# An attention-and-SwiGLU encoder layer on one core: adaLN partly on TensorE in the first wave, looser places for projection tiles, the last chunk's o tiles at other addresses

## The chip, the core and the metric

The kernel runs on one core of a Trainium2 chip. The core has five engines that run at the same time: TensorE (PE, matrix products; its weight loads are listed apart as PEld), VectorE (DVE), ScalarE (ACT), GpSimd (POOL) and SyncE (SP, which here only issues DMAs). They work on SBUF (128 partitions) and on PSUM, which has eight banks of 128 x 512 float32; PE writes PSUM. The metric is the device time of one execution in microseconds, the median of several runs.

## The reference, cut to what matters

One encoder layer: 2048 tokens of 1024 features, float32. A vector c is turned into six shift, scale and gate vectors; windowed attention and a SwiGLU FFN follow, each between two RMS norms.

```python
c_act = silu(c)
sh1, sc1, g1, sh2, sc2, g2 = split(c_act @ ada_w + ada_b, 6)
h = rmsnorm(x, mix_norm_pre) * (1 + sc1) + sh1
y = windowed_gqa_sink(h, w_qkv, w_o, sink, rel_bias)   # 16 heads, 4 kv heads, window 128
x = x + g1 * rmsnorm(y, mix_norm_post)
h = rmsnorm(x, ffn_norm_pre) * (1 + sc2) + sh2
a, b = split(h @ ffn_w_in, 2)                          # 2816 hidden
x = x + g2 * rmsnorm((silu(a) * b) @ ffn_w_out, ffn_norm_post)
```

## The kernel before, in words

The tokens lie along the free dimension in four chunks of 512; the 1024 features are eight tiles of 128 partitions (index k). Each float32 operand of a large product is split into a high part (a cast to a shorter float format, `hi`) and a rest (`lo`), and one product becomes three: hi·hi, hi·lo, lo·hi (`three`).

The order of stages is: a **first wave** for chunk 0, in which seven of the twelve 128-column groups of q, k and v are accumulated at once in seven PSUM banks over k; the other groups, chunk 1; then 64 attention units (4 chunks, 4 kv heads, 4 blocks of 128 queries), between which products of the q, k, v projection (first 32 units) and of the output projection for chunks 0 to 2 (last 32 units) are spread as filler; the output projection of the last chunk; then the FFN, by a Strassen-like scheme with seven products for two by two blocks. In the profile `k,q` are score products, `ident,pr` transposes of the probabilities, `phi,v` and `plo,v` value products, `ol,wo` output projection, `hb,w..`/`ht,w..` FFN.

For the first wave, each k needs a shift and a scale column (`mod`). Each column is one DVE reduction over a 128 x 1024 tile of ada_w against silu(c) broadcast to all partitions (`cb`); then x is multiplied by the norm factor r (`nr`), scaled and shifted on ACT, cast to `hi` on ACT, and `lo` is the difference on DVE. The weights come in raw tiles from a pool of five (`raws`), which the ada_w tiles share.

The program is not issued as written. A recorder (`Recorder`) takes all operations; a list scheduler (`forward`, `backward`, several rounds) orders them on each engine by its own estimates and gives each tile a place, and `emit` issues that order, so that all operations carry the line of `emit`. Tiles of one pool and tag share a number of places. `slot_of` gives a place only to the tile whose turn it is in the order in which the program first used the tag's tiles:

```python
t = b.tag
if t.order[t.next] is not b:
    return None
```

So with two places for (`psF`, `mm`), which hold output projections (`py`) and norm sums (`nst`) alike, a norm sum that is not ready holds up all projections behind it. After attention, SBUF that its pools had is given to the last chunk's output projection (`lasto`), from the top of the right side down in the order in which the pools are opened; attention's own pools began there with the bias tables, then q, k, v. A tile waits for the last reader of whatever lay at its address.

## Time and profile before

| | us |
|---|---|
| median of 3 runs | 2035.23 (2032.91 to 2036.42) |
| the profiled execution | 2033.44 |
| its span, first to last instruction | 2031.6 |
| PE busy | 1995.9 (98%) |
| DVE busy | 1689.8 (83%) |
| ACT busy | 1072.0 (53%) |
| POOL busy | 571.7 (28%) |

The chain that ended last is 65% PE. A group's or row's busy time counts overlapping matmuls once; a single matmul row is longer than the distance between two starts, because each drains while the next one runs. Rows of the timeline give start, length, engine, line, operation, tiles and shapes, and in brackets the idle time before it with what ended it.

### The profile page before, as it was taken

The page shows a single profiled execution, that of the slowest core. Times are in us where ns is not written, and L with a number is a line of the kernel's source. Part 1 is how long each engine was busy: PE and PEld are TensorE (multiplying, and loading weights), DVE is VectorE, ACT ScalarE, POOL GpSimd, SP SyncE. Part 2 cuts the span into 40 slices and gives each one's busy share as a digit, 9 for nine tenths or more (in the row PEclk, how much of TensorE's full clock was granted, in tenths as well). Part 3 has the DMA queues.
Part 4 walks back from the last instruction along what each step waited for, and adds up shares of the span by engine and source line. Part 5 has one row for each costly group of instructions (what it writes and reads, how often), then busy time and mean ns, then how long its engine had stood idle before and what let it go on. Part 6 is the DMA issues. An engine that isn't in the chain of part 4 may idle for free.

```text
span 2031.6 us, 29024 instructions
## 1 busy us (share of the span) xinstructions
PE 1995.9 (98%) x9392; PEld 1663.1 (82%) x9392; DVE 1689.8 (83%) x3051; ACT 1072.0 (53%) x2099; POOL 571.7 (28%) x520
## 2 busy tenths in 40 slices
PE   6999999999999999999999999999999999999999
PEld 4888888888787878788888888888888888888888
DVE  7868888877989888988887998776776789989997
ACT  5557766777778864344343533333333744455433
POOL 1302442344657513432333231111111000120034
PEclk9999999999999999999999999999999999999999
DMA  9895765576777694444446743333233794398543
GB/s 312 307 331 198 241 210 173 195 279 227 254 272 257 225 363 152 160 161 165 166 158 244 272 151 134 117 137 106 83 124 101 236 335 152 108 331 300 174 156 110
DMA packets 208581, 415.23 MB, mean 204 GB/s; under 512 B 19964, under 2 KB 61997, under 8 KB 205357
## 3 DMA queue, kind: packets, MB, share of 16 engines
q1 hardware_dynamic: 207852, 412.84, 59.1%
q8 instruction: 75, 1.23, 0.2%
q14 instruction: 78, 0.63, 0.1%
q10 hardware_dynamic: 576, 0.52, 0.1%
HBM read 278.52 MB, written 134.77 MB: 203 GB/s over the span
## 4 chain that ended last, share of the span: by engine, by line
PE 65%; DVE 2%; DMA 1%; issue 1%; ACT 0%; POOL 0%; SPq 0%; ACTq 0%; DVEq 0%; POOLq 0%
PE bank L748 65%; DMA hb<-h_d 0%; DVE pr L748 0%; DMA wor<-w_o 0%; DVE u_i L748 0%; DVE y L748 0%; DVE plo L748 0%; DMA ly<-y_d 0%; DMA lx<-xT 0%; DVE ly L748 0%; POOL ly L748 0%; DVE ws_i L748 0%; DVE wa_i L748 0%; SPq L748 0%; DVE of L748 0%
## 5 line engine op out<-in xcount | busy, mean ns | idle before, releaser
L748 PE MATMUL bank<-ht,ws_i 128*128 128x512 f32 x1584 | 374.0, 389 | 0.0
L748 PEld LDWEIGHTS bank<-ht,ws_i 128*128 128x128 f32 x1584 | 297.3, 188 | 61.7
L748 PE MATMUL bank<-hb,wa_i 128*128 128x512 f32 x1056 | 254.1, 389 | 0.5 <-DVE hb L748 0.5
L748 PEld LDWEIGHTS bank<-hb,wa_i 128*128 128x128 f32 x1056 | 198.1, 188 | 42.0 <-DVE hb L748 0.9
L748 PE MATMUL bank<-ol,wo 128*128 128x512 f32 x768 | 206.1, 396 | 2.1 <-ACT yacc L748 1.1
L748 DVE TENSOR_TENSOR u_i<-bank,u_i 128x512 f32<-128x512 f32 x176 | 120.9, 688 | 80.3 <-PE bank L748 77.7
L748 ACT CAST ws_i<-s_i 128x512 fp32r<-128x512 f32 x132 | 81.9, 621 | 192.9 <-DVE s_i L748 96.8
L748 ACT ACTIVATE pr<-pr,nm 128x385 f32<-128x385 f32 (+1 forms) x256 | 154.8, 606 | 53.2 <-DVE nm L748 48.0
L748 DVE CUSTOM_DVE_ANT_0 pr<-bank,bias,nsink 128x384 f32<-128x384 f32 (+1 forms) x256 | 149.8, 594 | 25.3 <-PE bank L748 21.7
L748 POOL TENSOR_SCALAR pr<-pr,rs 128x384 f32<-128x384 f32 (+1 forms) x177 | 114.6, 660 | 179.7 <-DVE rs L748 167.9
L748 PEld LDWEIGHTS bank<-ol,wo 128*128 128x128 f32 x768 | 141.2, 188 | 28.5 <-ACT yacc L748 1.5
L748 POOL TENSOR_TENSOR p_i<-p_i,u_i 128x512 f32<-128x512 f32 x41 | 66.9, 1633 | 346.3 <-DVE u_i L748 176.0
L748 POOL TENSOR_TENSOR z<-z,z 128x512 f32<-128x512 f32 x28 | 43.8, 1572 | 337.4 <-ACT ws_o L748 263.2
L748 PE MATMUL bank<-k,q 128*128 128x384 f32 (+1 forms) x512 | 135.4, 344 | 1.5 <-DVE nm L748 1.4
L748 PE MATMUL bank<-hi,ws 128*128 128x512 f32 x384 | 134.3, 400 | 0.0
L748 DVE TENSOR_TENSOR plo<-bank,phi 128x512 fp32r<-128x512 f32 x184 | 120.7, 684 | 11.2 <-ACT phi L748 10.1
L748 ACT CAST wa_i<-wiri 128x512 fp32r<-128x512 f32 x132 | 81.3, 620 | 90.8 <-PE bank L748 77.6
L748 PE MATMUL bank<-hb,ws_i 128*128 128x512 f32 x528 | 126.9, 389 | 1.6 <-ACT p_i L748 1.6
L748 PE MATMUL bank<-ht,wa_i 128*128 128x512 f32 x528 | 126.8, 389 | 0.0
L748 DVE TENSOR_TENSOR z<-bank,z 128x512 f32<-128x512 f32 (+1 forms) x164 | 107.7, 659 | 17.9 <-PE bank L748 16.5
L748 DVE TENSOR_TENSOR wa_i<-wiri,wa_i 128x512 fp32r<-128x512 f32 x132 | 103.8, 788 | 19.1 <-ACT wa_i L748 19.1
L748 PEld LDWEIGHTS bank<-hb,ws_i 128*128 128x128 f32 x528 | 99.0, 188 | 22.5 <-ACT p_i L748 2.0
(275 smaller groups left out, 4434.5 us busy)
## 6 DMA issues: line engine op xcount, KB each, us to landing
wiri<-w_in SPq DMA_DIRECT2D x88, 512.0 KB, 4.6
ada<-ada_w SPq DMA_DIRECT2D x40, 512.0 KB, 5.3
q_d<-e SPq DMA_DIRECT2D x32, 512.0 KB, 4.6
q<-q_d SPq DMA_DIRECT2D x16, 1024.0 KB, 7.0
wo<-wo_d SPq DMA_DIRECT2D x16, 1024.0 KB, 6.0
wiro<-w_out SPq DMA_DIRECT2D x40, 384.0 KB, 4.4
g_d_b<-p_i SPq DMA_DIRECT2D x44, 256.0 KB, 3.4
g_d_t<-p_i SPq DMA_DIRECT2D x40, 256.0 KB, 2.0
```

The costliest lines, as they stand in the source:

```text
L748: o.ins = getattr(engs[o.eng], o.fn)(*args, **kw)
```

## The change

- **First wave.** c also comes as eight columns (`ct`). For k = 0 the shift and the scale column are made by PE, eight products of one column each (`ada_products`, from a transposed copy of that part of ada_w), into a PSUM tile, and DVE adds the bias. The other k keep the DVE reduction. The ada_w tiles of the wave get a pool of their own with ten places (`raws0`), at the address of the second half of the weights, which opens after the wave. The split of the first half of the weights goes to DVE in the program instead of POOL. For chunk 0, `hi` is written by the scaling activation itself, the norm sum takes four partial sums instead of three, and its refinement is the short form (three DVE operations).
- **Warm products.** `busy` puts 14 products of 128 columns on `ones` at the start of PE's queue, six after the first partial sum, five on `t` and eight on `r` of the norm; nothing reads their result.
- **Loose places.** A tile may take a place ahead of up to four others of another name family (the leading letters of its name) for (`psF`, `mm`) and (`yp`, `nsq`). The y tiles of chunks 0 to 2 have 16 places instead of 12.
- **Last chunk.** The three pools of `lasto` are opened in another order: the o tiles first, so that they lie where the bias tables and the first q tiles lay, then weights, then y.

```diff
+ADA_PE = 1
+WARM = {"ones": 14, 0: 6, "t": 5, "r": 8}
+LOOSE = {("psF", "mm"): 4, ("yp", "nsq"): 4}
...
+            t.left = list(t.order)
+            skip = LOOSE.get((t.pool.name, t.name), 0)
+            t.reach = skip + 1
...
-            if t.order[t.next] is not b:
+            for x in t.left[:t.reach]:
+                if x is b:
+                    break
+                if x.family == b.family:
+                    return None
+            else:
                 return None
...
             for i, sq in enumerate(sums):
                 pe.matmul(ps, f(ones), sq, start=i == 0, stop=i == len(sums) - 1)
+                if fill is not None:
+                    fill(i, sq)
...
-            dve.tensor_tensor(sq[6], sq[4], sq[6], ALU.add)
-            self.acc = [sq[0], sq[2], sq[6]]
+            self.acc = sq[::2]
...
+            if c == 0:
+                act.activation(hi, xt, AF.Identity, bias=mod[:, k:k + 1], scale=coef[:, 0, k:k + 1])
+            act.activation(xt, xt, AF.Identity, bias=mod[:, k:k + 1], scale=coef[:, 0, k:k + 1])
+            if c == 0:
+                return scaled, dve.tensor_tensor(lo, xt, f(hi), ALU.subtract)
...
+        def ada_products(k):
+            for e, t in enumerate((8 + k, k)):
+                w = raws0.tile([P, D], F32, tag="raw", name=f"adat{t}")
+                sp.dma_start(w, a["ada_t"][t])
+                j = 2 * k + e
+                for i in range(KT):
+                    pe.matmul(ada_ps[:, j:j + 1], w[:, i * P:(i + 1) * P], ct[:, i:i + 1],
+                              start=i == 0, stop=i == KT - 1)
+                dve.tensor_tensor(mod[:, t:t + 1], ada_ps[:, j:j + 1], adab[:, t:t + 1], ALU.add)
...
-            split(t[:, 0], t[:, 1], w[:, :n], pool)
+            split(t[:, 0], t[:, 1], w[:, :n], pool if i else dve)
...
+        def busy(what, src):
+            for _ in range(WARM.get(what, 0)):
+                pe.matmul(warm[:, :P], f(ones), src[:, :P], start=True, stop=True)
...
-                y = yp.tile([P, CH], F32, tag="y", name=f"y{c}_{n}", bufs=4 if c == NCH - 1 else 12)
+                y = yp.tile([P, CH], F32, tag="y", name=f"y{c}_{n}", bufs=4 if c == NCH - 1 else 16)
...
+    op = open_pool(lasto, "op3", 4, side="right")
+    wop = open_pool(lasto, "wop3", 2, side="right")
     yp = open_pool(lasto, "yp3", side="right")
-    wop = open_pool(lasto, "wop3", 2, side="right")
-    op = open_pool(lasto, "op3", 4, side="right")
```

Since the scheduler orders everything anew, the change moves instructions on every engine. Three places follow.

PE at the very start, before (`nsq` are partial sums of squares, `hi` and `w` the operands of the first wave):

```order
L748 MATMUL bank0<-nsq0_0_86,ones_57 128x512
L748 MATMUL bank0<-nsq0_2_95,ones_57 128x512
L748 MATMUL bank0<-nsq0_6_115,ones_57 128x512
L748 MATMUL bank1<-hi0_0_164,w0_0_137 128x512
L748 MATMUL bank2<-hi0_0_164,w0_0_137 128x512
```

and now:

```order
L767 MATMUL bank0<-ones_57 128x128 x14
L767 MATMUL bank1<-nsq0_0_103,ones_57 128x512
L767 MATMUL bank0<-nsq0_0_103,ones_57 128x128 x6
L767 MATMUL bank1<-nsq0_2_114,ones_57 128x512
L767 MATMUL bank1<-nsq0_4_128,ones_57 128x512
L767 MATMUL bank1<-nsq0_6_138,ones_57 128x512
L767 MATMUL bank2<-mod_64,adat8_105 128x1 x8
L767 MATMUL bank2<-mod_64,adat0_112 128x1 x8
L767 MATMUL bank0<-nta0_175,ones_57 128x128 x5
L767 MATMUL bank0<-nr0_154,ones_57 128x128 x8
L767 MATMUL bank3<-hi0_0_206,w0_0_173 128x512
```

Sixteen one-column products and 13 warm ones now stand between the norm sum and the first product of the wave.

DVE in the same place, before, from the last sum of squares to the first `x` times r (`nr`; ISA rows on ada tiles are the reductions):

```order
L748 TENSOR_TENSOR nsq0_6_115<-nsq0_4_105,nsq0_6_115 128x512
L748 ISA ada8_93,mod_132<-ada8_93,cb_84,adab_88 128x1024
L748 ISA mod_132 128x1
L748 ISA ada0_98,mod_132<-ada0_98,cb_84,adab_88 128x1024
L748 ISA mod_132 128x1
L748 TENSOR_TENSOR w0_0_137<-wqkv0_0_103,w0_0_137 128x896
L748 SCALAR_TENSOR_TENSOR nta0_143<-bank0,nta0_143 128x512
L748 ISA ada1_113,mod_132<-ada1_113,cb_84,adab_88 128x1024
L748 ISA mod_132 128x1
L748 TENSOR_SCALAR nta0_143<-nta0_143 128x512
```

and now:

```order
L767 TENSOR_TENSOR mod_64<-bank2,adab_101 128x1
L767 SCALAR_TENSOR_TENSOR nta0_175<-bank1,nr0_154 128x512
L767 SCALAR_TENSOR_TENSOR nta0_175<-nta0_175,nr0_154 128x512
L767 SCALAR_TENSOR_TENSOR coef_186<-mod_64,gains_131 128x1
L767 SCALAR_TENSOR_TENSOR nr0_154<-nta0_175,nr0_154 128x512
L767 TENSOR_TENSOR w0_0_173<-wqkv0_0_119,w0_0_173 128x896
L767 TENSOR_TENSOR x0_0_71<-x0_0_71,nr0_154 128x512
L767 TENSOR_TENSOR mod_64<-bank2,adab_101 128x1
L767 ISA ada9_136,mod_64<-ada9_136,cb_126,adab_101 128x1024
L767 ISA mod_64 128x1
L767 ISA ada1_141,mod_64<-ada1_141,cb_126,adab_101 128x1024
L767 ISA mod_64 128x1
```

Three reductions no longer stand among the norm's steps; an add that reads PE's modulation bank stands ahead of them, and two reductions follow `x` times r.

PE in the second half of attention, around the norm of chunk 0's new x (`nhix0`; `wo1_n` are projection tiles of chunk 1), before:

```order
L748 MATMUL bank7<-plo9_3_2_5721,v2_3_5120 128x512
L748 MATMUL bank4<-ident_59,pr10_3_5513 128x128
L748 MATMUL bank5<-ident_59,pr10_3_5513 128x128
L748 MATMUL bank6<-ident_59,pr10_3_5513 128x128
L748 MATMUL bank3<-k3_0_5308,q3_0_5301 128x384 x2
L748 MATMUL bank2<-k3_0_5308,q3_0_5301 128x384 x2
L748 MATMUL bank1<-nhix0_5747,ones_57 128x512
L748 MATMUL bank0<-ol1_0_4217,wo1_4_5528 128x512 x4
```

and now:

```order
L767 MATMUL bank0<-ol1_3_5126,wo1_4_5548 128x512 x3
L767 MATMUL bank1<-ol1_0_4261,wo1_5_5671 128x512 x6
L767 MATMUL bank1<-ol1_1_4281,wo1_5_5671 128x512 x3
L767 MATMUL bank3<-k3_0_5363,q3_0_5353 128x384 x2
L767 MATMUL bank1<-ol1_1_4281,wo1_5_5671 128x512 x3
L767 MATMUL bank5<-ident_59,pr10_3_5574 128x128 x2
L767 MATMUL bank6<-ident_59,pr10_3_5574 128x128 x2
L767 MATMUL bank4<-ident_59,pr10_3_5574 128x128
L767 MATMUL bank1<-ol1_2_5097,wo1_5_5671 128x512
L767 MATMUL bank2<-k3_0_5363,q3_0_5353 128x384 x2
L767 MATMUL bank1<-ol1_2_5097,wo1_5_5671 128x512 x2
L767 MATMUL bank0<-nhix0_5837,ones_57 128x512
```

Projection tile 4 and most of tile 5 have moved ahead of the norm sum.

PE after attention's last value product (`plo15_3_1`; `ol3_n` are the last chunk's o tiles, `hb` the FFN's), before:

```order
L748 MATMUL bank7<-plo15_3_1_7249,v3_3_6684 128x512
L748 MATMUL bank0<-ol2_2_6043,wo2_6_7032 128x512
L748 MATMUL bank0<-ol2_3_6068,wo2_6_7032 128x512 x6
L748 MATMUL bank1<-ol2_0_5132,wo2_7_7174 128x512 x6
L748 MATMUL bank1<-ol2_1_5218,wo2_7_7174 128x512 x6
L748 MATMUL bank1<-ol2_2_6043,wo2_7_7174 128x512 x6
L748 MATMUL bank1<-ol2_3_6068,wo2_7_7174 128x512 x6
L748 MATMUL bank0<-ol3_0_7136,wo3_0_6868 128x512 x6
```

and now:

```order
L767 MATMUL bank7<-plo15_3_1_7328,v3_3_6769 128x512
L767 MATMUL bank1<-ol2_1_5271,wo2_7_7050 128x512 x3
L767 MATMUL bank1<-ol2_2_6070,wo2_7_7050 128x512 x6
L767 MATMUL bank1<-ol2_3_6101,wo2_7_7050 128x512 x6
L767 MATMUL bank0<-ol3_0_6628,wo3_0_7268 128x512 x6
```

Fewer products of chunk 2 are left for after attention. From the last row shown to the first product on `ol3_3` there are 36 more products before and 31 now: 73 and 52 in all.

More of the change, by code (lines that the diff above doesn't have):

```diff
@@ L2 @@
 import random
+import re
 from contextlib import ExitStack
@@ L92, in __init__ @@
         self.log, self.ops, self.slot, self.real = [], set(), None, None
+        self.group, self.family = None, re.match("[a-z]*", name).group()
 class Tag:
@@ L193, in record @@
             op.reads.append(op.writes[0])
-        elif fn == "matmul":
+        elif fn == "matmul" and op.writes[0][0].group is None:
             op.writes = [(op.writes[0][0], (3, (1 << P) - 1))]
@@ L218, in record @@
                     op.tiles.append(b)
+        if eng == "pe" and op.writes[0][0].group is not None:
+            for q in op.writes[0][0].group:
+                op.pred.setdefault(q, 0)
+            op.writes[0][0].group = [op]
         op.succ = []
@@ L262, in cost @@
             elif outs[0].dtype == F32 and ins[0].dtype == F32:
-                op.occ, op.lat = 860 * n // CH, 1060 * n // CH
+                op.occ, op.lat = max(860 * n // CH, 230), max(1060 * n // CH, 400)
             else:
@@ L545, in forward @@
                     t.next += 1
+                    t.left.remove(b)
                     wake(t)
@@ L754, in f, with columns @@
     return ap.bitcast(F32)
+def columns(nc, ap):
+    b = nc.bufs[ap.tensor.name]
+    b.unit, b.group = 1, []
 def row(ap, n):
@@ L800, in encoder_layer @@
     gains = constr.tile([P, 4, KT], F32, name="gains")
+    ct = mod[:, 6 * KT:7 * KT]
     nsink = const.tile([P, HEADS], F32, name="nsink")
@@ L808, in encoder_layer, with rstd_of @@
     pool.custom(lambda nc, t: make_identity(nc, t), ident)
-    def rstd_of(alloc, psp, ptag, acc, tag, r=None, direct=False, short=False, keep=False):
+    def rstd_of(alloc, psp, ptag, acc, tag, r=None, direct=False, short=False, keep=False, fill=None):
         sums = acc if isinstance(acc, list) else [acc]
@@ L834, in rstd_of @@
             dve.scalar_tensor_tensor(out, t, 1.5, r, ALU.add, ALU.mult)
+            if fill is not None:
+                fill("t", t)
+                fill("r", r)
             return out
@@ L889, in squares0, with norm @@
                     dve.tensor_tensor(sq[k - 1], sq[k - 1], sq[k], ALU.add)
-            dve.tensor_tensor(sq[6], sq[4], sq[6], ALU.add)
-            self.acc = [sq[0], sq[2], sq[6]]
-        def norm(self, psp, ptag):
+            self.acc = sq[::2]
+        def norm(self, psp, ptag, fill=None):
             r = nrm.tile([P, CH], F32, tag="nr", name=f"nr{self.c}")
-            self.r = rstd_of(rot(nrm, "nsq", 2), psp, ptag, self.acc, f"a{self.c}", r)
+            self.r = rstd_of(rot(nrm, "nsq", 2), psp, ptag, self.acc, f"a{self.c}", r,
+                             short=self.c == 0, fill=fill)
         def h(self, k):
@@ L899, in h @@
             scaled = dve.tensor_tensor(xt, xt, self.r, ALU.mult)
-            act.activation(xt, xt, AF.Identity, bias=mod[:, k:k + 1], scale=coef[:, 0, k:k + 1])
             hi = hs.tile([P, CH], F32R, tag="hi", name=f"hi{c}_{k}")
@@ L937, in encoder_layer @@
     with ExitStack() as pa:
-        w2 = open_pool(pa, "w2", side="right")
         raws = open_pool(pa, "raws", 5, side="right")
         w1 = open_pool(pa, "w1", side="right")
+        first = ExitStack()
+        raws0 = open_pool(first, "raws0", KT * C2 * 2 // D, side="right")
         psA = open_pool(pa, "psA", 8, space=PSUM)
         cb = nrm.tile([P, D], F32, name="cb")
+        sp.dma_start(ct, a["ct"])
         sp.dma_start(cb, row(a["c"], D))
@@ L947, in encoder_layer @@
         sp.dma_start(gains, a["gains"])
+        act.activation(ct, ct, AF.Silu)
         act.activation(cb, cb, AF.Silu)
@@ L957, in ada_reduce @@
             dve.tensor_tensor_reduce(w, w, cb, 1.0, adab[:, t:t + 1], ALU.mult, ALU.add, mod[:, t:t + 1])
+        ada_ps = psA.tile([P, CH], F32, tag="mm", name="ada_ps")
+        columns(nc, ada_ps)
+        def ada_products(k):
[7 more added lines that the diff above has]
+                dve.tensor_tensor(mod[:, t:t + 1], ada_ps[:, j:j + 1], adab[:, t:t + 1], ALU.add)
         wres = {}
         def w_piece(k, i):
-            pl, lo_c, n = ((w1, 0, C1), (w2, C1, C2))[i]
+            pl, lo_c, n = (w2, C1, C2) if i else (w1, 0, C1)
             w = raws.tile([P, D], F32, tag="raw", name=f"wqkv{k}_{i}")
@@ L970, in w_piece @@
                 wres[k, "v"] = (t[:, 0, :2 * P], t[:, 1, :2 * P])
+        warm = psA.tile([P, CH], F32, tag="mm", name="warm")
+        def busy(what, src):
+            for _ in range(WARM.get(what, 0)):
+                pe.matmul(warm[:, :P], f(ones), src[:, :P], start=True, stop=True)
+        busy("ones", f(ones))
         ch0.squares0()
-        ch0.norm(psA, "mm")
+        ch0.norm(psA, "mm", busy)
         steps = []
@@ L976, in encoder_layer @@
         for k in range(KT):
-            ada_reduce(*ada_load(8 + k, raws))
-            ada_reduce(*ada_load(k, raws))
+            if k < ADA_PE:
+                ada_products(k)
+            else:
+                ada_reduce(*ada_load(8 + k, raws0))
+                ada_reduce(*ada_load(k, raws0))
             dve.scalar_tensor_tensor(coef[:, 0, k:k + 1], mod[:, 8 + k:9 + k], 1.0, gains[:, 0, k:k + 1],
@@ L984, in encoder_layer @@
                 three(pss[n], wres[k, n], ch0.hh[k], k == 0, k == KT - 1)
+        first.close()
+        w2 = open_pool(pa, "w2", side="right")
         for n in NORD[:WAVE]:
@@ L1833 @@
         "ada_w": np.asarray(ada_w)[0].T.reshape(6 * KT, P, D),
+        "ada_t": np.asarray(ada_w)[0].reshape(KT, P, 6 * KT, P)[:, :, :KT + ADA_PE].transpose(2, 1, 0, 3)
+        .reshape(KT + ADA_PE, P, D),
+        "ct": np.asarray(c).reshape(KT, P).T,
         "ada_b": cols(ada_b[0]),
```

## The prediction

> **What bounds the kernel now.** I read the page's first part, then what PE waited for, then engine times by stretches cut at those waits, then the timeline at each.

> ```profile
> span 2031.6 us, 29024 instructions
> PE 1995.9 (98%) x9392; PEld 1663.1 (82%) x9392; DVE 1689.8 (83%) x3051; ACT 1072.0 (53%) x2099; POOL 571.7 (28%) x520
> ...
> PE bank L748 <- DVE nsq L748: 9.1, 3, 5.8
> PE bank L748 <- ACT hi L748: 8.1, 1, 8.1
> PE bank L748 <- DVE lo L748: 3.1, 2, 2.4
> ...
> 0.00:23.40 23.40, 6.19 (x7) 1.51 (x7) 12.45 (x24) 14.91 (x19) 2.04 (x7) 1.00 0.92 329
> 23.40:26.40 3.00, 3.00 (x7) 2.29 (x8) 3.00 (x4) 1.69 (x2) 1.59 (x1) 1.00 0.70 194
> 26.40:66.00 39.60, 36.35 (x152) 28.89 (x152) 35.52 (x49) 20.75 (x30) 14.95 (x8) 0.96 0.88 287
> 66.00:540.00 474.00, 472.68 (x2514) 405.79 (x2513) 384.68 (x902) 332.67 (x740) 162.51 (x199) 1.00 0.71 241
> 540.00:565.00 25.00, 21.98 (x100) 16.99 (x99) 21.46 (x51) 16.09 (x38) 18.38 (x16) 0.86 0.87 288
> 565.00:630.00 65.00, 65.00 (x349) 55.93 (x348) 55.98 (x140) 53.99 (x122) 34.38 (x43) 1.00 0.72 238
> 630.00:660.00 30.00, 28.03 (x149) 22.35 (x148) 29.65 (x73) 24.88 (x63) 24.89 (x28) 1.00 0.90 299
> 705.00:717.00 12.00, 9.47 (x38) 6.61 (x37) 10.17 (x15) 7.78 (x13) 0.59 (x1) 1.00 1.05 405
> 717.00:1990.00 1273.00, 1271.44 (x5604) 1051.53 (x5604) 1069.94 (x1659) 546.02 (x965) 269.59 (x176) 1.00 0.52 181
> ```

> In the stretches the columns are length, busy time of PE, PEld, DVE, ACT and POOL, PE's granted clock, DMA share and GB/s. From 66 us on TensorE is the bound, so time is to be had only where it idles or runs slowly. It idles 1.3 us in 66 to 540, 3.0 in 540 to 565, nothing to 630, 2.0 to 660, 2.5 in 705 to 717, and 1.6 in the 1273 us after. The start is the large piece:

> ```profile
> 8.47 3.21 ACT L748 ACTIVATE nsq<-x 128x512 f32<-128x512 f32 x5 [2.35 <-DMA x<-xT]
> 13.29 2.04 PE L748 MATMUL bank<-nsq,ones 128*128 128x512 f32 x2 [1.33 <-DVE nsq L748]
> 14.09 1.28 DVE L748 CUSTOM_DVE_ANT_0 ada<-ada,cb,adab 128x1024 f32<-128x1024 f32 x1 [0.95 <-ACT cb L748]
> 15.30 0.08 DVE L748 DVE_READ_ACCUMULATOR2_ANT mod<- 128x1 f32 x1
> 15.37 0.69 ACT L748 ACTIVATE nr<-bank,epsc 128x512 f32<-128x512 f32 x1
> 16.84 0.63 ACT L748 ACTIVATE nr<-nr 128x512 f32<-128x512 f32 x1
> 16.96 1.09 DVE L748 TENSOR_TENSOR w<-wqkv,w 128x896 fp32r<-128x896 f32 x1 [0.37 <-ACT w L748]
> 18.16 0.69 DVE L748 SCALAR_TENSOR_TENSOR nta<-bank,nta 128x512 f32<-128x512 f32 x1
> 21.89 0.81 ACT L748 ACTIVATE x<-x,mod,coef 128x512 f32<-128x512 f32 x1
> 23.40 3.25 PE L748 MATMUL bank<-hi,w 128*128 128x512 f32 x7 [8.07 <-ACT hi L748]
> 29.47 1.98 PE L748 MATMUL bank<-hi,w 128*128 128x512 f32 x8
> 45.55 3.21 DVE L748 CUSTOM_DVE_ANT_0 ada<-ada,cb,adab 128x1024 f32<-128x1024 f32 x1
> 46.00:48.00 2.00, 0.99 (x5) 0.48 (x3) 2.00 (x1) 0.83 (x1) 1.68 (x1) 1.00 0.81 233
> 48.00:50.00 2.00, 0.57 (x2) 0.48 (x3) 2.00 (x4) 1.26 (x3) 1.09 (x1) 1.00 0.81 229
> ```

> The first wave (168 products of the first chunk) begins at 23.40. Its first seven products take 3.25 us where eight later ones take 1.98, so PE starts at half its speed: 1.4 us lost by 26.40. From there to 66 us it idles 39.60 - 36.35 = 3.25 us, and the mean clock of 0.96 stands for 0.04 x 39.6 / 0.5 = 3.2 us at half clock, 1.6 lost. **Lost at the start: 23.4 + 1.4 + 3.25 + 1.6 = 29.6 us.**

> **The start, after the change.** A small DMA (c by columns) now leads SP's queue; I take 0.6 us for it, and move x by that much. The squares of x end at 8.47 + 3.21 = 11.7, now 12.3. One DVE sum (0.69, as every step on 512 columns) brings 13.0; the further sum of sums is gone, PE adds four instead. The last norm product took 2.04 us, two passes of 1.02 at half clock; at full clock I take half and a little, 0.9, so 13.9. Full clock needs the warm products: 14 from about 1 us on, each two passes of 128 columns, a quarter of 1.02 us each: 28 x 0.25 = 7 us of work, and then six more among the norm products.

> Logarithm and exponential (0.69, 0.63) give 15.3. But in DVE's order the tiny add of the first modulation column stands ahead of the norm's steps, and it waits for eight products of two passes (priced below at 0.11 each): 13.9 + 1.7 + 0.2 = 15.8. Three DVE steps at 0.69 (the short form; a square on ACT is gone) give 17.9. The split of the first weights, next on DVE, takes 1.09, x times r 0.69, the second tiny add 0.1, then hi comes straight from the activation in 0.81, its 0.62 us cast gone: 20.6. c by rows is now behind the first weights on SP's queue: 4.1 MB ahead and with it, at 329 GB/s 12.5 us, so landed by about 16; its silu (table load and 1.06 us) ends before DVE asks for it at 19. Ten PSUM tiles share eight banks there; the last two wave tiles follow the norm's and the modulation's, both read by 19.

> In front of hi PE's queue now carries 16 one-column products and 13 warm ones, 58 float32 passes:

> ```profile
> 535.80 0.60 PE L748 MATMUL bank<-ident,pr 128*128 128x128 f32 x4
> 550.80 0.27 PE L748 MATMUL bank<-ident,pr 128*128 128x128 f32 x1
> ```

> No row shows a one-column product. These are nearest: a float32 pass of 128 columns with its own weight load starts every (0.60 - 0.27) / 3 = 0.11 us. 58 x 0.109 = 6.3 us end at 20.2, just ahead of hi. Bounds: 0 (hi comes at 20.0, by the exponential) and 0.25, the pass at half clock (13.9 + 14.5 = 28.4). I take 0.109, because the load is the same 128 columns. [...]

> Then the pace per k. DVE: two reductions at 1.21 (15.30 less 14.09), w 1.09, x and lo 0.69 each, 4.9 us, 4.8 with the 0.1 by which rows overlap. PE: 21 x 0.227 = 4.8 (29.47's row: 1.98 less 0.39 of pipe, over 7). DMA: 1.5 MB, at 329 GB/s 4.6 us. Even, then, with 0.4 us at the first lo (DVE does two reductions ahead of it) and 1 us over the other rounds. POOL leaves the wave: the reduction of 3.21 us instead of 1.28 ran while POOL split w. If DVE is late, the second weight half's V products stand ahead of the last round. **Lost after: 20.6 + 0.4 + 1.0 = 22.0; gain 7.6** (0 with passes at 0.25, 9.6 with no slip and hi at 20.0).

> **The middle.**

> ```profile
> 550.83 0.47 PE L748 MATMUL bank<-ol,wo 128*128 128x512 f32 x1
> ...
> 555.11 0.61 PE L748 MATMUL bank<-ident,pr 128*128 128x128 f32 x3 [1.25 <-DVE pr L748]
> 556.82 1.12 PE L748 MATMUL bank<-ident,pr 128*128 128x128 f32 x4 [1.11 <-POOL pr L748]
> ...
> 563.42 0.50 PE L748 MATMUL bank<-nhix,ones 128*128 128x512 f32 x1 [0.20 <-DVE nhix L748]
> 563.76 1.10 PE L748 MATMUL bank<-ol,wo 128*128 128x512 f32 x4
> ```

> No projection product (ol,wo) runs from 550.83 to 563.76: the second norm's tile (nhix) holds the next place in the two-bank order, so PE has attention alone, some 5.3 us of products in 13 us. The stretch idles 3.0 us, and its clock of 0.86 stands for 0.14 x 25 / 0.5 = 7.0 us at half, 1.2 of them idle, 2.9 lost: 5.9 in all. With loose places and 16 y tiles, two projection tiles precede that norm in PE's order, and the longest run without projection falls from 5.3 to 3.9 us of products. Such a run of 3.6 us stands in the stretch 66 to 540, which idles 1.3 us in all. I leave 1.5: gain 4.4, bounds 0 and 5.9. In 630 to 660 DVE is busy 29.65 of 30 us, so that loss stays.

> ```profile
> o_d<-of SPq DMA_DIRECT2D x64, 128.0 KB, 3.0
> ol<-o_d SPq DMA_DIRECT2D x16, 512.0 KB, 5.1
> 692.27 0.39 PE L748 MATMUL bank<-plo,v 128*128 128x512 f32 x1
> 711.70 2.56 PE L748 MATMUL bank<-ol,wo 128*128 128x512 f32 x10 [0.71 <-DVE ol L748]
> 715.34 4.83 PE L748 MATMUL bank<-ol,wo 128*128 128x512 f32 x20 [1.08 <-ACT yacc L748]
> ```

> The last chunk's fourth o tile is first read 73 products after attention's last one, and 52 after it in the changed order: 16.6 and 11.8 us of cover. Its chain (o stored, loaded, split) took 19.4 us, 692.27 to 711.70, in a crowded queue; at median landings it is about 2 + 3.0 + 5.1 + 2.3 = 12.4. Three of the four tiles come earlier now, which thins that queue. So a wait of 0.6 to 7.6; I take 2, near the medians, where before it was 1.5 with the FFN's; and the 1.08 for a bank should go, since FFN products now stand between. Gain 0.6, bounds -5 and 2.5.

> **Sum:** 7.6 + 4.4 + 0.6 = 12.6 us off the profiled execution's 2033.4: 2020.8. That one lies 1.8 us below the median of the runs shown, which spread over 3.5; I forecast **2021.5**, between the two readings, and set the rivals by it.

> **Rivals.** (1) The middle's stall only moves. Projection work is spent earlier, DVE is full at 630 to 660 already, and units there wait what was saved: middle gain 0, 2026. (2) The start falls short: the 58 passes average 0.18 us, partly at half clock, the first product comes at 24.3, and the gain is 4: 2025. For it: what half clock there is in 26.40 to 66 follows 46 to 50, though PE worked 1.6 of those four us, so gaps among the norm products could drop it. [...] (3) Slower. After the second chunk's norm PE's order has 3.9 us of bare attention and then four units (16.3 us) with only 33 projection products (7.5 us). At the bare pace of 550 to 563, 13 us for 5.3 or 2.45 times, these 20.2 us take 49.5 against 27.7 of PE work, 21.8 lost against 2.0 now: 2041 with the 12.6 gained. It decides from a pace of about 2.2. Against it: in 565 to 630 attention with projection kept PE full.

> **Chances.** Forecast 0.60 (its own range 2014 to 2027), stall moves 0.22, start falls short 0.12, slower 0.06. Less than 0.2%, 4 us, cannot be told from no change here. Faster 0.59 + 0.19 + 0.10 = 0.88, same 0.07, slower 0.05. Range 2012 to 2030: down to the best bounds (9.6 + 5.9 + 2.5 is 2016, and 2.9 us idle elsewhere), up to rivals 1 and 2 with the worst wait for the o tile.

> **What would show it.** First hi product between 20 and 21.5 us, seven in 2.0 us; no DVE reduction above 1.3 us before 45; PE idle under 2.5 us from there to 60. No stretch over 8 us without ol,wo and no clock of 0.50 between 530 and 600. The fourth o tile waits 0 to 4 us. I am wrong if the first product comes after 24 us, or if PE idles over 8 us between 600 and 700.

## The result and the profile after it

The changed kernel takes **2018.51 us** (median of 4 runs, 2017.22 to 2020.18) against 2035.2 for the kernel before: a ratio of 0.9919, 95% interval 0.9904 to 0.9933, so 16.5 us less by the ratio (13.6 to 19.5 by its interval) and 16.7 between the medians. The forecast was 2021.5, in a range of 2012 to 2030. Its profiled execution took 2017.89 with a span of 2016.1, 15.5 less than the profiled execution of before, where the prediction's sum had 12.6.

The stretches of the changed kernel (columns as in the prediction: length, busy time of PE, PEld, DVE, ACT and POOL, PE's granted clock, DMA share, GB/s):

```profile
16.00:18.00 2.00, 1.94 (x9) 1.94 (x10) 1.97 (x6) 1.99 (x2) 0.00 (x0) 0.50 1.03 419
18.00:20.00 2.00, 2.00 (x10) 2.00 (x11) 2.00 (x5) 0.58 (x2) 0.00 (x0) 0.50 1.04 424
23.00:63.00 40.00, 39.58 (x186) 33.01 (x185) 38.44 (x56) 24.16 (x34) 10.88 (x6) 1.00 0.86 317
63.00:540.00 477.00, 475.86 (x2535) 410.48 (x2534) 388.26 (x914) 336.85 (x747) 164.86 (x202) 1.00 0.70 241
540.00:565.00 25.00, 25.00 (x134) 21.15 (x132) 21.74 (x51) 18.89 (x46) 17.80 (x19) 1.00 0.88 309
630.00:660.00 30.00, 29.53 (x162) 24.56 (x162) 27.77 (x73) 27.38 (x67) 23.58 (x33) 1.00 0.85 286
690.00:717.00 27.00, 24.55 (x99) 19.24 (x99) 22.36 (x29) 16.90 (x27) 5.80 (x4) 0.94 1.03 385
717.00:1975.00 1258.00, 1257.43 (x5543) 1039.78 (x5542) 1059.65 (x1651) 540.92 (x951) 261.80 (x169) 1.00 0.51 178
```

Where PE lost 3.0 us of idle time and 14% of its clock before (540 to 565), it now never idles and the clock is whole. In 23 to 63 us it idles 0.42. But ahead of the first wave the clock stands at 0.50 while PE is busy, and in 690 to 717 PE still idles 2.45 us and runs at 0.94.

To compare runs whose order differs, I use one measure throughout: what a stretch **loses** is its length less its products at full pace (0.227 us for 512 columns, 0.175 for 384, 0.120 for 256, 0.109 for 128: the median distance from one start to the next in the kernel before, where the row of one 512-column product alone is 0.39 us long). Norm, modulation and warm products ahead of the wave don't count as work. It takes in idle time and half clock alike. Gains are taken before rounding; in the two long stretches the losses hang on the last digit of these paces, their differences do not.

| Stretch, us | before | after | gain | forecast gain |
|---|---|---|---|---|
| 0 to 66 | 30.9 | 24.2 | 6.7 | 7.6 |
| 66 to 540 | 7.3 | 6.2 | 1.2 | none |
| 540 to 660 | 12.5 | 3.3 | 9.3 | 4.4 |
| 660 to 720 | 4.4 | 5.4 | -1.1 | 0.6 |
| 720 to the end | 11.2 | 11.8 | -0.6 | none |

The start as the changed kernel ran it (the timeline of PE and of ACT: start, length, operation, count, and idle time before it):

```profile
13.60 2.21 PE L767 MATMUL bank<-mod,adat 128*128 128x1 f32 x18
16.06 3.15 PE L767 MATMUL bank<-mod,adat 128*128 128x1 f32 x14 [0.25 <-DVE mod L767]
19.07 2.48 PE L767 MATMUL bank<-nta,ones 128*128 128x128 f32 x10
19.77 0.81 ACT L767 ACTIVATE hi<-x,mod,coef 128x512 fp32r<-128x512 f32 x1 [1.42 <-DVE mod L767]
21.35 2.36 PE L767 MATMUL bank<-nr,ones 128*128 128x128 f32 x16
23.46 1.85 PE L767 MATMUL bank<-hi,w 128*128 128x512 f32 x7
```

`hi` was ready at 19.77 + 0.81 = 20.58, the 20.6 of the forecast. But the first product on it starts at **23.46**, where it started before (23.40): PE was still at the 58 passes of one-column and warm products, which took 9.9 us from 13.60 on, not 6.3. The last chunk's fourth o tile, as PE waited for it:

```profile
692.80 0.73 PE L767 MATMUL bank<-ol,wo 128*128 128x512 f32 x2 [1.92 <-ACT ol L767]
694.06 2.05 PE L767 MATMUL bank<-ol,wo 128*128 128x512 f32 x5 [0.53 <-DVE ol L767]
```

2.45 us of waiting, and half clock behind it: five products take 2.05 us at 694.06, where eight took 1.98 at 29.47 in the kernel before.

So the total came out near the sum while its parts did not. Three questions follow: why the first product was late, why the start gained all the same, and what the middle's gain is due to.

### The profile page after: what moved, and what is told of

Same layout as the page of the kernel before. It is cut to its first block, busy times and chain, and to the rows that moved or that the text cites. A ratio compares the mean times of both kernels' runs of the same rounds, so it can differ in the third digit from the quotient of the medians.

```text
span 2016.1 us, 29153 instructions
## 1 busy us (share of the span) xinstructions
PE 2001.9 (99%) x9492; PEld 1677.9 (83%) x9492; DVE 1684.7 (84%) x3045; ACT 1077.0 (53%) x2100; POOL 563.6 (28%) x523
## 5 line engine op out<-in xcount | busy, mean ns | idle before, releaser
L767 DVE CUSTOM_DVE_ANT_0 pr<-bank,bias,nsink 128x384 f32<-128x384 f32 (+1 forms) x256 | 150.0, 595 | 23.8 <-PE bank L767 19.6
L767 POOL TENSOR_TENSOR z<-z,z 128x512 f32<-128x512 f32 x31 | 50.1, 1626 | 327.2 <-DVE z L767 215.4
L767 POOL TENSOR_TENSOR p_i<-p_i,u_i 128x512 f32<-128x512 f32 x34 | 55.7, 1640 | 305.0 <-DVE u_i L767 187.3
L767 ACT CAST phi<-bank 128x512 fp32r<-128x512 f32 x184 | 102.0, 588 | 28.9 <-PE bank L767 27.6
## 6 DMA issues: line engine op xcount, KB each, us to landing
wiri<-w_in SPq DMA_DIRECT2D x88, 512.0 KB, 4.7
ada<-ada_w SPq DMA_DIRECT2D x38, 512.0 KB, 7.2
q_d<-e SPq DMA_DIRECT2D x32, 512.0 KB, 3.3
```

The costliest lines, as they stand in the source:

```text
L767: o.ins = getattr(engs[o.eng], o.fn)(*args, **kw)
```

## Experiments on the start

All edits are to the changed kernel unless said otherwise. Each edit lets the planner lay out the whole program anew, so the text reads stretches, and the totals with care. The stretches are those of one profiled execution of each run; e4's took 2.5 us more than that run's median, e1's 1.9 more and e11's 2.2 less.

| Run | time, us | first hi product | 0 to 66 | 160 to 200 | 540 to 660 | 660 to 720 |
|---|---|---|---|---|---|---|
| before | 2035.2 | 23.40 | 30.9 | 0.6 | 12.5 | 4.4 |
| after | 2018.51 | 23.46 | 24.2 | 0.5 | 3.3 | 5.4 |
| e1 128-column passes | 2017.97 | 20.80 | 24.3 | 0.5 | 3.3 | 5.5 |
| e2 no warm products behind the norm | 2018.75 | 20.52 | 24.1 | 0.5 | 3.3 | 4.9 |
| e11 no warm products | 2021.45 | 19.78 | 23.4 | 0.5 | 3.5 | 6.1 |
| e3 modulation on DVE | 2025.04 | 23.16 | 29.5 | 5.2 | 1.7 | 7.0 |
| e5 e1, V's high part on ACT, low part left out | 2016.8 | 19.90 | 21.2 | 3.5 | 2.8 | 3.6 |
| e6 V's high part on ACT, low part left out | 2017.77 | 21.91 | 21.9 | 3.3 | 3.0 | 3.4 |
| e9 e1, V split in two | 2019.94 | 19.92 | 21.1 | 6.7 | 2.8 | 3.8 |
| e4 strict places, 12 y | 2030.9 | 23.94 | 24.3 | 4.5 | 13.8 | 5.6 |
| e7 strict places, 16 y | 2025.26 | 21.07 | 23.1 | 2.0 | 12.9 | 4.1 |
| e8 old order of the last pools | 2023.19 | 23.45 | 24.1 | 4.7 | 3.5 | 8.3 |
| e10 before with loose places | 2031.62 | 26.50 | 35.5 | 1.0 | 3.0 | 9.9 |
| e12 e9, another planner number | 2016.15 | 19.59 | 20.6 | 0.4 | 5.2 | 4.1 |

**e1: does the one-column form cost the clock?** The order of every engine is the same as in the changed kernel; only the width that a pass streams differs.

```diff
-pe.matmul(ada_ps[:, j:j + 1], w[:, i * P:(i + 1) * P], ct[:, i:i + 1], ...)
+pe.matmul(ada_ps[:, j * P:(j + 1) * P], w[:, i * P:(i + 1) * P],
+          ct[:, i:i + 1].to_broadcast([P, P]), ...)
```

> Edit: the 16 one-column products of the first modulation read the same column 128 times, so each pass streams 128 columns instead of 1; the order of every engine is the same as in the changed kernel. Theory A (the clock follows the columns that are streamed: a one-column pass counts as idle): the granted clock stays 1.00 from 14 to 22 us, the 58 passes take 0.11 each, the first hi product starts at about 20.6, when hi itself is ready (20.58 in the changed kernel), and the time falls by 2.9 us to 2015.6. Rival B (the clock falls some 10 us after it rose, whatever the products are): it falls near 15.3 again, the first hi product starts at 23.4, and the time stays at 2018.5.

Two of its stretches:

```profile
16.00:18.00 2.00, 1.77 (x15) 1.77 (x16) 1.95 (x5) 1.97 (x3) 0.00 (x0) 1.00 1.02 413
18.00:20.00 2.00, 2.00 (x20) 2.00 (x19) 2.00 (x5) 0.62 (x2) 0.00 (x0) 1.00 1.02 418
```

and PE's timeline:

```profile
16.23 1.83 PE L767 MATMUL bank<-mod,adat 128*128 128x128 f32 x14 [0.25 <-DVE mod L767]
17.90 1.28 PE L767 MATMUL bank<-nta,ones 128*128 128x128 f32 x10
20.80 1.89 PE L767 MATMUL bank<-hi,w 128*128 128x512 f32 x7
...
56.74 0.39 PE L767 MATMUL bank<-w,hi 128*128 128x256 f32 x1 [0.91 <-DMA wqkv<-w_qkv]
60.73 0.38 PE L767 MATMUL bank<-w,hi 128*128 128x256 f32 x1 [1.40 <-POOL w L767]
```

The clock stays at 1.00, 14 passes take 1.83 us in place of 3.15, and the first hi product comes at 20.80, right after `hi`: theory A for the clock. Across the runs it holds without exception. The clock fell during the passes or just behind them in all seven runs with one-column passes (after, e2, e4, e6, e7, e8, e11: 0.50 to 0.77 in 16 to 18 us); it stayed at 1.00 in all four with 128 columns (e1, e5, e9, e12).

Gaps in PE's work are the other possible cause, and the traces' clock records speak to it. In all of them a stretch of one granted clock lasts a whole multiple of 3.41 us (10.24 at full, then 6.83 at half in the changed kernel), save the last, which the kernel's end cuts off. So each fall can be set beside the 3.41 us ahead of it, here the changed kernel's two:

```profile
11.96:15.37 3.41, 3.21 (x21) 2.26 (x19) 0.62 (x1) 2.73 (x4) 0.00 (x0) 1.00 1.00 398
691.21:694.62 3.41, 1.29 (x4) 0.78 (x5) 1.84 (x3) 2.91 (x5) 0.06 (x1) 1.00 1.05 412
```

Leaving out the one when each kernel ends, fourteen falls in these runs have no one-column passes ahead of them, and there PE was busy 0.47 to 1.96 of the 3.41 us, as in the second row. At the seven behind one-column passes it was busy 3.08 to 3.21, as in the first, with 1.8 us or more of it in these passes. So gaps do not explain these seven.

**And the time did not fall.** Most of the 2.7 us were given back at 56.74 and 60.73 (0.91 and 1.40), where the first V products wait for the second weight halves. e1 loses 24.3 to 66 us, the changed kernel 24.2. So theory A was right on the clock and wrong on the time, and so was the prediction's step that counts the first product's time in full.

**e2 and e11: the same from the other side.** The warm products behind the norm left out (e2), or all of them (e11):

```diff
-WARM = {"ones": 14, 0: 6, "t": 5, "r": 8}
+WARM = {"ones": 14, 0: 6, "t": 0, "r": 0}    # e2;  e11: WARM = {}
```

> Edit: the 13 warm products (26 passes) between the one-column products and hi are left out; those ahead of and among the norm sums stay. Theory A (PE's queue, not hi, sets the first hi product, and the one-column products have dropped the clock): PE is free at 19.2, the first hi product starts at 20.6 with hi, but at half clock, its first seven take 3.2 us and the half clock lasts some 4 us, so 2 us are lost again: equal to a start at 22.6, time 2017.6. Rival B (the warm products are what gives the wave its full clock, and without them the clock stays low through the first rounds with gaps): over 3 us lost at half clock, time 2020 or more.

> Edit to the changed kernel: no warm products at all. Theory A (the first wave's end is set by what stands behind it, not by the first product or its clock): the norm's sums and the one-column passes run at half clock, the first hi product comes at about 22.4 and its first 4 us run at half clock, but 0 to 66 us loses 24 to 25, against 24.2, time 2018 to 2020. Rival B (the warm products carry the gain of the start): 0 to 66 loses 27 or more, time 2021.5 or more.

In e2 the first product came at 20.52 with its first seven at half clock (3.32 us), as expected, but the stretch lost 24.1, no better. In e11 it came at 19.78, at half clock too, and the stretch lost 23.4, a little less than either theory had. The norm did not end later without warm products either: the first modulation pass started at 12.90 (13.60 in the changed kernel), since the norm's own products brought the clock up on the way (two passes of 512 columns in 2.07 us at 6.68, two in 1.13 at 11.94). So the 33 warm products show no gain in this phase. e11's time of 2021.45 is above the changed kernel's, but its profile is of its fastest execution, with a span of 2017.4, so it does not show where the others lost more.

**e5, e6: take the V splits off POOL.** In the changed kernel POOL splits second weight halves back to back, 2.0 us each:

```profile
50.97 1.94 POOL L767 TENSOR_TENSOR w<-wqkv,w 128x640 fp32r<-128x640 f32 x1 [49.66 <-DMA wqkv<-w_qkv]
54.05 10.03 POOL L767 TENSOR_TENSOR w<-wqkv,w 128x640 fp32r<-128x640 f32 x5 [1.15 <-DMA rb<-rel_bias]
```

```diff
-split(t[:, 0], t[:, 1], w[:, :n], pool if i else dve)
+if i:
+    act.copy(t[:, 0], w[:, :n])
+    act.copy(t[:, 1], w[:, :n])
+else:
+    split(t[:, 0], t[:, 1], w[:, :n], dve)
```

> Edit: the 128-column passes of e1, and the low halves of the second weight halves are left out: ACT writes the high half twice, where POOL subtracted (so the V and last QKV products are without their low weight part; 0.8 us on ACT in place of 2.0 on POOL). Theory A (the end of the first phase is set by POOL's splits of the second weight halves, back to back at 2.0 us from 54 to 64 us, so that an earlier first product is given back there): PE no longer waits at 56 to 61 us, and 0 to 66 us loses 21.5 to 22 in place of the 24.3 of e1. Rival B (the loads of those halves set it: one landed only at 56.87): PE still waits for the load there, and 0 to 66 loses 23 to 24.3.

> Edit: as e5, but with the one-column passes of the changed kernel. Theory A (there the late first product and POOL's splits end together, by chance): the first hi product stays at 23.4 and 0 to 66 us loses 23.8 to 24.2, little better than the changed kernel's 24.2; e5 beats it by the 2.4 us or more that the clock held saves. Rival B (the late first product costs nothing in any case): e5 and e6 lose the same within 0.5 us.

Both write the high part twice and have no low part of these weights, so they only show what the split costs.

```profile
54.00:58.00 4.00, 4.00 (x19) 3.34 (x18) 0.87 (x2) 3.96 (x8) 0.00 (x0) 1.00 0.82 202
58.00:62.00 4.00, 4.00 (x29) 3.73 (x29) 0.00 (x0) 4.00 (x7) 0.00 (x0) 1.00 1.02 406
```

In e5 (above, two of its stretches) PE has no wait left at 54 to 62 us and the start loses **21.2**: theory A. The load that e1 waited 0.91 for is no longer waited for either, which fits a load held up by the splits that free its place. In e6 the first product came at 21.91 and not at 23.4, because the clock fell later there (0.77 in 16 to 18 us where the changed kernel has 0.50), and it lost 21.9. Its expectation missed for that reason. The result lies between its two theories: a first product 2.0 us earlier, in e5, is worth 0.7. In e6 nothing is lost behind the first product (21.91 and 21.9). In e5 it is 1.3 (19.90 and 21.2), most of it one wait for `lo`:

```profile
22.73 0.50 PE L767 MATMUL bank<-lo,w 128*128 128x512 f32 x1 [0.95 <-DVE lo L767]
```

With 2.0 us splits on POOL and the modulation on PE, the loss is 23.1 to 24.3 wherever the first product stands between 19.78 and 23.94.

**e3: what the products on PE are worth.**

```diff
-ADA_PE = 1
+ADA_PE = 0
```

> Edit: the first modulation column goes back to two DVE reductions (no one-column products); warm products, split on DVE, short rstd and places stay. Theory A (the one-column products cost more than they save): the two reductions (1.28 us each) lie in DVE's idle time before the norm's steps, hi is ready by 20 to 21, the clock is not dropped by one-column passes, first hi product between 20 and 21.5, time about 2016. Rival B (the reductions lie on the path to hi, which was the point of moving them): first hi product 2.5 us later than hi was ready, 23 us or later, time 2018.5 to 2021.

Both theories missed. The timeline of ACT:

```profile
20.11 0.81 ACT L767 ACTIVATE hi<-x,mod,coef 128x512 fp32r<-128x512 f32 x1 [2.99 <-DVE x L767]
```

of PE:

```profile
17.80 2.50 PE L767 MATMUL bank<-nta,ones 128*128 128x128 f32 x10 [4.63 <-DVE nta L767]
23.16 1.86 PE L767 MATMUL bank<-hi,w 128*128 128x512 f32 x7
```

and two stretches:

```profile
54.00:58.00 4.00, 1.33 (x7) 0.73 (x6) 4.00 (x5) 3.97 (x7) 3.62 (x3) 0.88 0.65 206
58.00:62.00 4.00, 3.98 (x11) 3.31 (x12) 4.00 (x3) 3.03 (x5) 4.00 (x3) 0.50 0.76 250
```

`hi` is ready at 20.92, only 0.34 later than with the products on PE, so the two reductions did fit ahead of the norm's steps as theory A had it. The first product is late for another reason, the warm products at half clock behind 4.63 us of idle PE. And the 5.3 us that e3 loses against the changed kernel arise from 54 us on: PE waits 2.66 us for POOL's splits of V's weights (1.26 and 1.40) and then runs at 0.50, from 57.08 to 63.91 by the clock record. Waits of 0.91 and 1.40 at the same place in e1 were not followed by half clock. So in this pair of runs the products on PE did not pay ahead of the wave's first product; whether the loss at its end is theirs or that of an order that came out anew is not shown. The other 4.7 us of e3's longer time stand at 160 to 200, in the first attention units, whose order came out anew.

**e9: a split that keeps the whole result.** V needs 256 of a second half's 640 columns, so these are split first:

```diff
-split(t[:, 0], t[:, 1], w[:, :n], pool if i else dve)
+for s in (slice(0, 2 * P), slice(2 * P, n)) if i else (slice(0, n),):
+    split(t[:, 0, s], t[:, 1, s], w[:, s], pool if i else dve)
```

> Edit: the 128-column passes of e1, and each second weight half is split in two steps, first its 256 V columns, then the other 384, so that V's products wait for a shorter step. Nothing is left out. Theory A (POOL's 2.0 us splits set the end of the first phase): V's products wait for steps of about 0.9 us, the waits of 0.91 and 1.40 of e1 shrink to under 0.5 in all, 0 to 66 us loses 21.5 to 22.5 in place of 24.3, and if the rest of the order loses what the changed kernel lost, the time is 2016. Rival B (POOL's total, now longer by eight starts, or the loads decide): 0 to 66 loses 24 or more, time 2018 or more.

The start lost 21.1, so theory A again. But the time was 2019.94 and not 2016: 160 to 200 us lost 6.7 in place of 0.5. That stretch of e9 idles 2.80 us and has a clock of 0.91:

```profile
160.00:200.00 40.00, 37.20 (x179) 31.05 (x178) 32.16 (x84) 29.61 (x70) 10.59 (x17) 0.91 0.66 227
```

and PE's timeline has the wait in it:

```profile
170.57 1.22 PE L767 MATMUL bank<-k,q 128*128 128x256 f32 x4 [2.56 <-DVE nm L767]
171.95 2.73 PE L767 MATMUL bank<-k,q 128*128 128x384 f32 x6 [0.16 <-DVE nm L767]
```

Ten score products stand together there with no filler between them, wait for DVE, and half clock follows (six of them take 2.73 us).

## Experiments on the middle and the last chunk

**e4, e7, e10: is it the places?** e4 takes back loose places and y buffers, e7 the places alone, e10 adds both to the kernel before and nothing else.

```diff
-LOOSE = {("psF", "mm"): 4, ("yp", "nsq"): 4}
+LOOSE = {}
-bufs=4 if c == NCH - 1 else 16
+bufs=4 if c == NCH - 1 else 12               # e4 only
```

> Edit: places are taken in strict order again and y has 12 buffers; the new start and the new pool order of the last chunk stay. Theory A (the loose places gave the middle's gain): PE's order has bare attention of 6.9 us around the first norm and of 10.2 us around the second (5.3 and 5.0 in the kernel before, which lost 7.2 and 4.5 there), so 540 to 660 loses 12 us or more against 3.3 in the changed kernel: time 2028 to 2036. Rival B (the middle's gain came with the earlier start, which shifted the schedule): time within 3 us of 2018.5.

> Edit: places in strict order again, but y keeps its 16 buffers. Theory A (the order rule gives the middle's gain, not the buffers): PE's order has 7.4 and 7.7 us of bare attention before the two norms, and 540 to 690 us loses 10 or more beyond the changed kernel, as in e4: 2027 to 2033. Rival B (the four more y buffers give it, since a waiting projection tile needs one): time within 3 us of 2018.5.

> Edit to the kernel before: only the loose places and 16 y buffers; its old start and its old pool order stay. Theory A (they alone give the middle's gain): 540 to 660 us loses 3 to 5 in place of 12.5, 0 to 66 stays at about 31, time 2035 less 8 to 9, so 2026 to 2027. Rival B (they need the rest of the change): 540 to 660 loses 9 or more, time 2031 or more.

The same two stretches of e4, e7 and e10, in that order:

```profile
540.00:565.00 25.00, 22.04 (x95) 16.46 (x94) 22.54 (x55) 16.72 (x40) 17.93 (x19) 0.86 0.88 289
630.00:660.00 30.00, 28.01 (x145) 21.64 (x143) 26.11 (x69) 23.83 (x56) 24.48 (x26) 1.00 0.87 287
```

```profile
540.00:565.00 25.00, 22.86 (x106) 17.66 (x105) 21.70 (x52) 18.44 (x44) 18.94 (x22) 0.93 0.70 244
630.00:660.00 30.00, 27.22 (x142) 21.22 (x141) 28.25 (x68) 25.76 (x61) 25.73 (x30) 1.00 0.82 277
```

```profile
540.00:565.00 25.00, 25.00 (x132) 20.97 (x132) 22.66 (x53) 19.63 (x46) 20.36 (x19) 1.00 0.79 260
630.00:660.00 30.00, 29.18 (x162) 24.77 (x161) 28.52 (x75) 24.76 (x63) 24.09 (x26) 1.00 0.89 297
```

Theory A in all three. With strict places both stretches lose again, whether y has 12 buffers (13.8 in 540 to 660) or 16 (12.9); with loose places on the old kernel they lose 3.0. The buffers alone bring nothing there. Loose places with 12 buffers were not tried, so whether the rule needs the 16 stays open. The totals of e7 and e10 missed their bounds. e7's 2025.26 is below the 2027 to 2033 expected: its start lost 1.1 less than the changed kernel's, its last chunk 1.3 less, and from 720 us on it lost 2.5 less. e10's 2031.62 is above 2026 to 2027: its start came out 4.6 worse (first hi product at 26.50) and its last chunk 5.5 worse. The middle's 9.5 us were won, and most of them given away by the new order elsewhere.

**e8: the last chunk's pools.**

```diff
-op = open_pool(lasto, "op3", 4, side="right")
-wop = open_pool(lasto, "wop3", 2, side="right")
 yp = open_pool(lasto, "yp3", side="right")
+wop = open_pool(lasto, "wop3", 2, side="right")
+op = open_pool(lasto, "op3", 4, side="right")
```

> Edit: the last chunk's pools go back to their old order (y, weights, o tiles). Theory A (the fourth o tile's chain of store, load and split ends the last chunk's start in either order, with 11.6 us of cover against 12.0): PE waits 2 to 3 us for it again and runs some 4 us at half clock, 660 to 720 us loses 5 to 6.5, time 2018 to 2020. Rival B (the new order lets three tiles come earlier and so thins the queue): with the old order the fourth tile lands later and 660 to 720 loses 8 or more, time 2021 or more.

```profile
689.13 1.43 PE L767 MATMUL bank<-ol,wo 128*128 128x512 f32 x5 [0.37 <-DVE wo L767]
691.37 0.96 PE L767 MATMUL bank<-ol,wo 128*128 128x512 f32 x3 [0.80 <-DVE ol L767]
...
697.63 2.56 PE L767 MATMUL bank<-ol,wo 128*128 128x512 f32 x10 [1.42 <-DVE wo L767]
700.67 1.20 PE L767 MATMUL bank<-ol,wo 128*128 128x512 f32 x4 [0.48 <-ACT ol L767]
702.81 3.47 PE L767 MATMUL bank<-ol,wo 128*128 128x512 f32 x14 [0.94 <-DVE ol L767]
```

660 to 720 loses 8.3 in place of 5.4: rival B's number, though not its mechanism. PE waits at several places, twice for a weight tile's split on DVE and not only for the fourth o tile, and the clock stays whole. In this pair the new order of the pools is 2.9 us better there. That this is the pools' doing is not shown: with the new order the stretch loses anything from 3.4 (e6) to 7.0 (e3), and with the old one 4.4, 8.3 and 9.9 (before, e8, e10). Another 4.2 of e8's longer time stand at 160 to 200, which the pools' order touches only through the planner, and from 720 us on e8 loses 2.9 less than the changed kernel.

**e12: can the start's gain be kept?** One number of the planner's, on top of e9:

```diff
-SPARE = 800.0
+SPARE = 1000.0
```

> Edit to e9 (128-column passes, second weight halves split in two steps): one number of the planner's, SPARE, goes from 800 to 1000, which gives another order after the first phase. Nothing is left out. In this order no bare run of attention is longer than 1.0 us in the first 14 us of attention (1.9 in e9, 1.8 at 13.5 us in the changed kernel), and none longer than 2.8 us around the two norms. Theory A (what e9 saved at the start was given back only by the order of the first attention units, which came out anew): 0 to 66 us loses 21 to 22 as in e9, 160 to 200 loses under 1.5 in place of 6.7, 540 to 660 under 3, time 2013 to 2016. Rival B (the first attention units wait for something that an earlier start doesn't bring earlier): 160 to 200 loses 3 or more again, time 2017 or more.

160 to 200 lost 0.4 and the start 20.6, as theory A had it, while 540 to 660 lost 5.2, more than expected. The time, just above theory A's bound, is 2016.15 us (2015.46 to 2017.56), a ratio of 0.9912 to the kernel before (0.9899 to 0.9926). That is the lowest median of all, but the interval overlaps the changed kernel's, so a gain over it is not shown.

## Why the prediction was right, and where it was not

**The start (7.6 forecast, 6.7 measured).** Right in its sum by luck, through two errors against each other.
- "20.6" for the first product was `hi`'s time (20.58), but not PE's: the term "58 x 0.109 = 6.3 us" was 9.9, 0.17 a pass. The price of a one-column pass was right: 0.11 us at full clock, 0.21 at half (14 in 3.15 us). The 0.6 us for the column DMA was an estimate that no run shows: the squares of x ended at 11.85, 0.17 later than in the kernel before. What failed is that the clock would hold. Rival 2 had the number (0.18 a pass, first product at 24.3), but as a consequence of gaps among the norm products; e1 shows that it was the one-column passes.
- The other error: I let the first product's time count in full. Up to it the change gained nothing (23.40 and 23.46); behind it the stretch lost 7.5 before and 0.7 after, 6.8 us, where "0.4 + 1.0" against 6.2 had 4.8. e1, e2 and e11 show that an earlier product would have added at most 0.8 to it, since POOL's V splits end the phase.

Of the 7.5 us, 4.4 lay in 46 to 54 us, and they are gone. There two of the kernel before's reductions took 3.21 and 3.12 us while POOL split w; the changed kernel, whose POOL splits nothing before 50.97, has no reduction above 1.28 (lowest, median and highest in ns):

```profile
L748 DVE CUSTOM_DVE_ANT_0 ada<-ada,cb,adab x16: 1271/1276/3208, 14.1 to 56.8; 128x1024 f32<-128x1024 f32 x16
L767 DVE CUSTOM_DVE_ANT_0 ada<-ada,cb,adab x14: 1272/1278/1283, 19.6 to 53.8; 128x1024 f32<-128x1024 f32 x14
```

That fits the prediction's "POOL leaves the wave", but is not tested alone: before, a reduction at 21.76 kept its 1.28 us although POOL split from 22.06 on. The wave's edits were not taken back one by one either, so the share of each in the 6.8 us is not shown; the warm products (e11) have none that can be seen.

By instruction times PE was busy 1.81 of 2 us and more from 14 us on, and the clock fell all the same, at 15.37. With the same passes 128 columns wide (e1) it stayed at 1.00: the width decided here, by what mechanism is not shown.

**The middle (4.4 forecast, 9.3 measured).** The mechanism held (e4, e7, e10); the term was mis-sized twice. In 540 to 565 I left 1.5 of 5.9; the loss by the measure used here was 7.2, and 0.6 stayed. And "that loss stays", said of 630 to 660 because DVE was busy 29.65 of 30 us, was wrong: it fell from 4.5 to 1.9. DVE's full row did not set that loss: with strict places e4 and e7 lose 4.5 and 5.8 there with DVE busy 26.11 and 28.25 us, and loose places alone (e10) bring it to 1.7 with 28.52. The bare run of attention at the second norm came from the same strict places. Rival 1, the stall that moves to that stretch, is refuted there, and so is rival 3: PE lost 1.9 us in 630 to 660 and 0.6 in 660 to 690, not 21.8.

**The last chunk (0.6 forecast, -1.1 measured).** The wait for the fourth tile was 2.45 us, where I took 2. So it saved almost nothing against the 2.53 us that PE idled in 705 to 717 before. What I left out is the half clock behind that wait, 3.41 us of it from 694.62 on. How much that cost can be read from e2, whose order is the changed kernel's from 57 us on. It waited as long at the same place and kept its clock:

```profile
693.43 0.73 PE L767 MATMUL bank<-ol,wo 128*128 128x512 f32 x2 [1.84 <-ACT ol L767]
694.70 1.43 PE L767 MATMUL bank<-ol,wo 128*128 128x512 f32 x5 [0.53 <-DVE ol L767]
```

It lost 4.9 in place of 5.4, since a wait of 0.64 for an `hb` tile came up instead. So without the half clock, too, the term would have been a loss of 0.5 and not a gain of 0.6.

**Elsewhere** (66 to 540, and from 720 on) the two programs differ by 0.6 in all, with no term for it in the sum.

## What to carry to other kernels

A busy engine row next to a falling clock is worth a look at the shape of what runs: with passes that load weights and stream one column in its queue, PE was busy 3.08 to 3.21 of the 3.41 us ahead of each of seven falls here. Before pricing an earlier start, look for what the end of the phase waits for: three ways to start the first product 2.7 to 3.7 us earlier brought less than 1 us while POOL's splits stood at the end. And where a planner lays out the whole program, read an edit at its own stretch: loose places alone won 9.5 us in the middle, and the total showed 2.5.
